# A hybrid decoder layer on one core: another table of turns, and buffers laid out in the order of the record

## The chip, the cores and the metric

The kernel runs on one core of one Trainium2 chip. A core has five engines that run at the same time, each through its own list of instructions strictly from front to back: TensorE (PE in the profile, with its weight loads shown as PEld), VectorE (DVE), ScalarE (ACT), GpSimd (POOL) and SyncE (SP), which here does nothing but issue DMA transfers. An instruction that needs another engine's result, or a buffer that another engine still uses, waits at the head of its list, and everything behind it on that engine waits too.

The metric is device time in microseconds (us) of one execution. A difference of under 0.2% is taken as no change.

## The reference

One layer of a decoder with two groups of heads side by side, 1024 tokens of width 1024, one batch, float32:

```python
h = rms_norm(x, attn_norm_w)
proj = h @ w_in                                  # 1024 x 4496, split into the columns below
(a_q, a_k, a_v, a_z, a_b, a_a, b_q, b_k, b_v, b_z, i_q, i_k, i_w) = split(proj)

# group A: gated DeltaNet, 4 heads of 128
qkv = silu(causal_dwconv([a_q, a_k, a_v]))       # 4 taps
beta, g = sigmoid(a_b), -exp(a_log) * softplus(a_a + dt_bias)
o_a = gated_delta_rule_chunked(l2(a_q), l2(a_k), a_v, g, beta)   # chunks of 64 tokens
o_a = rms_norm(o_a) * silu(a_z)

# group B: sparse attention, 8 heads of 64 over 2 key/value heads
score[t, s] = sum_h i_w[t, h] * relu(i_q[t, h] . i_k[s])         # 8 indexer heads of 128
keep the 256 best causal keys of each token
o_b = softmax(rms(b_q) . rms(b_k) / 8 over the kept keys) @ b_v * silu(b_z)

x = x + [o_a, o_b] @ w_out
gate = sigmoid(rms_norm(x) @ w_gate + b_gate)
x = x + (p @ w_ple) * gate                       # p: 1024 x 256, w_ple: 256 x 1024
```

## The kernel before, in words

**Stages.** The work runs through these stages, which overlap at their borders. In the *head* (about the first 60 us) the input x and a transposed copy of it are loaded in eight blocks of 128 tokens (`xt`, `xc`), each block is normalized, and the product p @ w_ple is formed meanwhile and stored to DRAM in sixteen pieces (`plt` stored to `pled`). Then come the projection columns as a stream of jobs, with the indexer's scores, the search for the 256 best keys and the DeltaNet chunks as chains of work between them. At about 520 us the sparse attention starts, with the rest of the projections and the output projection run between its steps. The last stretch is the second half of the output projection, the gate and the output.

**Products in three passes.** Every large product is made of three matmuls in a rounded format: each operand is split into a high part and a low part, and high x high, low x high and high x low are summed. For a weight piece of 128x512 the raw load is `raww`, the high part `hiw` (cast by ACT, or by DVE for the first piece), the low part `low` (a subtraction on POOL). For p they are `phi` (ACT) and `plo` (DVE, lines 858 to 863), for the normalized x `hThi` and `hTlo`. The product itself is `mm` in PSUM; `ple_out` (lines 878 to 888) copies it to `plt` on ACT and has SP store it.

**Attention.** `kv_load` (lines 1761 to 1767) brings the keys `kst` in eight transfers of 128 tokens each and the values `vst` in one; `load_q` (lines 1777 to 1787) brings the queries of one block of 128 tokens as `Qt`, one transfer, and splits them: ACT writes the two high halves of `qT`, DVE the two low halves. The score product `S` (line 1808) takes `qT` and `kst`, DVE turns it into the masked logits `P` and their minimum `mn`, ACT takes the exponential.

**The end of attention.** The attention's last outputs are transposed and scaled (`ot`), and ACT and POOL split them into `mch` and `mcl` (allocated in `tail_open`, line 1893). These are operands of the output projection's second part, jobs `body` in `out_job` (line 1944), whose result is `g` for the second half of the tokens.

**What sets the order.** None of the calls above reaches an engine at once. `Plan` records each as an `Op` with the earlier ops that it depends on, and each buffer's birth as a mark. `Plan.run` (line 486) then takes the ops in the order that the table `TURNS` gives: 7,561 numbers, packed as text, each the place of the next op among those not yet taken. `Plan.issue` (line 537) issues them in that order, so the table fixes the order of every engine's list, SP's transfers included. Since all recorded work is issued by line 557, the profile shows that line for everything, and one reads it by the names of tiles. The waits between engines come from the dependences and, where a buffer takes memory that another buffer had before, from that reuse.

**Where buffers lie.** A `LatePool` knows all of its buffers when it opens. `lay` sorts them and allocates one after the other; those that hold product operands and fill whole lines of 512 bytes come first, then the rest, and padding keeps the pools' borders on such lines. Which pool's buffer covers which bytes of an earlier pool, and so who waits for whom at reuse, hangs on this order.

Of the kernel before, what the change touches and what calls it, by code (L numbers as in the profile page):

```python
# [79 lines left out]
=7!C{1<aBOxZS|z0!}AzIDp;m1~!`wSY5VEr~H`HSnXCzz6F@gK+5q*mMqC>j+lESNpe{vbDMdoO_EwYlG*IEOLjXjSxnXTI<w6rm0QX!rV_KM&?;F>W|IU=*(OnvU#3Xd  # L80
WHKA&5_}m(lgS92CX>!3&bMH`4Q9Jszd_LJwI+?;Xw+wCXInJ7cwEv&qZ**eH0XjsjY$JCGSmi(pckAb!6pi@+F;U)^H8f@S~;^$2A^e$$KzT)8r4SNuqHE8PzT|FnimA8
!1J8dYUc!tQ4*BAp4TEun+6sHmXGr$o;R>6ol2!vDL9pjb30vDr^4Y-*kPMwu|yQGlqpFeCSYPR5Rqo}T2|}U!Wy-jf*1p%Cyg||Os^mqo?#eP{wX7hpDP%Kq-omnQ<`>5
H0O{w&d70`mZJ?opeTl+Xa!9xm4reL%YO(PMR_TbBw3a<u&ka?DvfGVq0n-2!E#|7I}Zh;n1`fNi3$ayRLWt7QQfOm!Kmf~GUTkZ{DEW$g+fQlr3>V;Wi&x$Q51#AZK5-2
x|^m^it3PK2tp79f*>S<z;OePY2-v0L9j%l97*`(e2eCrh00Xv=^Axr`2NqGuX}rIJ@$+j?7_?+$W+7HZ@>1@*yPv3Z+!o!p`ZOj-`4BR#h>WH?MDg1LlhBtxD!vJm<`Lu
P&6)~Xao(j=sl3A8kK8DS(Qpq@jS0msa#quYv<KgtJ<PAn^{S!udkQ6GbW9Wj+(2hC3b~>*yUm)^XzdJrJX8AjzeWvB@;H4Rb{b+Rc4hGRGIuLpBTJH5U0uEa*0lt#c6d|
?elE2S_j?B@4*^bX$yz7W@|7QwCKWeuuYqjBQ?p$&K4WoS@Y;32D<wDHL++f))VO-F2tDmtc6AQP<anaD?2)(6>a$fO7q;duC5fjOtI-FKjD77Rz`b4Tie9M<m8!&)2BCI
xIjOB5&qjHqf3^YTXOdN#J84=d&VZmn3E^Jdzv}re)0?>zs{V=+$KM$(>D$DldsdXidG-zKK!tc>Fs5D&h^kMR-9h3YSpTvM^_y|mK{F)`pQF(KKkgD70#nakt4KPeO<2O
I7^?qb!*?vORpcnGEmeY<IW?`zxw?1uShRneesPK@0#zvAie&&^yZu9L$~knuSze!^2&h&FTM5}dFMs`?p<>4>#ALEzWEn-cHKS5yz<H$uiSn2-48yv`yXz8_2y0XyZc|=
zkmO?_fy)vq~W4w&S2O`>E5JnpM8b;i2smcDdjvqxPANf`CI3ybJwX?zk%~--h1!mGcVo2UVZgF=JqF_;MXqESFgTy@$Qw2fA@E{uiv?Q_wLP`|K;YJH(y}B%G|tkhrY4q
# [2175 lines left out]
```

## Time and profile before

The median of three runs is 816.04 us (815.69 to 816.8). The profiled execution took 816.13 us; its records span 814.4 us.

| engine | busy us | share of the span |
|---|---|---|
| PE (matmul) | 802.3 | 99% |
| PEld (weight load, beside PE) | 685.0 | 84% |
| DVE | 615.7 | 76% |
| ACT | 572.6 | 70% |
| POOL | 493.2 | 61% |

The DMA engines move 93.14 MB at a mean of 114 GB/s. TensorE's mean granted clock is 0.998 of full speed.

How to read the rows further down: in a timeline each row has its start, its length (both in us), the engine, the line, the operation and `out<-in`; `xN` at the end means N like instructions in one row, and a bracket shows for how long the engine had been idle ahead of it and what ended that. The rows of SP are the issuing of transfers, not their landing. In a table of windows each row has its stretch of time and its length, then the busy time of each engine with its count, TensorE's granted clock, the share of the DMA engines that was busy, and GB/s. Matmuls are pipelined: a 512 wide one is shown with a length of 0.39 us but the next one starts about 0.23 us later, so lost time is read from the starts.

### The profile page before, as it was taken

The numbers are of one execution on the slowest core, as the hardware profiler recorded it, in microseconds if no ns is written. First come the engines' busy times: TensorE is split into PE (matmuls) and PEld (weight loads), VectorE is DVE, ScalarE is ACT, GpSimd is POOL, SyncE is SP. The second block draws the span as 40 slices with busy tenths as digits, with TensorE's granted clock in tenths as the row PEclk, the third lists the DMA queues.
The fourth block names the chain that finished last, engine by engine and source line by source line (L and its number), as shares of the span: only waits on it lengthen the run. The fifth ranks groups of instructions, "written<-read, shape, count | busy, mean of one in ns | idle before, by whom it ended". The sixth has DMA issues, their size and how long they took to land.

```text
span 814.4 us, 14745 instructions
## 1 busy us (share of the span) xinstructions
PE 802.3 (99%) x5111; PEld 685.0 (84%) x5111; DVE 615.7 (76%) x1420; ACT 572.6 (70%) x1317; POOL 493.2 (61%) x670
## 2 busy tenths in 40 slices
PE   8999999999999999999999999999999999999996
PEld 6898889888888888888888888887888888788885
DVE  4654446756778889989999988798868898686577
ACT  6753565555568978988999985498766789886342
POOL 3433514223235765767678775758875478899982
PEclk9999999999999999999999999999999999999999
...
GB/s 289 380 190 105 80 76 53 69 94 65 43 36 38 89 96 55 82 55 103 103 61 48 109 102 104 234 116 234 181 148 137 78 66 52 183 63 79 155 193 130
DMA packets 77866, 93.14 MB, mean 114 GB/s; under 512 B 24000, under 2 KB 40672, under 8 KB 77664
## 3 DMA queue, kind: packets, MB, share of 16 engines
...
## 4 chain that ended last, share of the span: by engine, by line
PE 90%; DMA 3%; ACT 3%; DVE 2%; POOL 1%; issue 1%; SPq 0%; ACTq 0%
PE mm L557 53%; PE g L557 9%; PE s L557 6%; PE lg L557 6%; PE pv L557 4%; PE S L557 4%; PE pt L557 4%; PE rec L557 3%; PE po L557 2%; DMA xt<-in_x_dram 2%; DMA pled<-plt 1%; ACT P L557 1%; DMA Qt<-qd 1%; POOL rs L557 0%; SPq L557 0%
## 5 line engine op out<-in xcount | busy, mean ns | idle before, releaser
L557 POOL TENSOR_TENSOR low<-raww,hiw 128x512 fp32r<-128x512 f32 (+1 forms) x109 | 145.5, 1339 | 130.3 <-ACT hiw L557 124.7
L557 PE MATMUL mm<-hTlo,hiw 128*128 128x512 f32 (+1 forms) x528 | 196.6, 382 | 0.0
L557 PE MATMUL mm<-hThi,hiw 128*128 128x512 f32 (+1 forms) x528 | 195.8, 383 | 0.0
L557 PE MATMUL mm<-hThi,low 128*128 128x512 f32 (+1 forms) x528 | 194.4, 381 | 0.0
L557 PEld LDWEIGHTS mm<-hThi,low 128*128 128x128 f32 x528 | 99.1, 188 | 16.9
L557 PEld LDWEIGHTS mm<-hThi,hiw 128*128 128x128 f32 x528 | 99.1, 188 | 16.1
L557 PEld LDWEIGHTS mm<-hTlo,hiw 128*128 128x128 f32 x528 | 98.9, 188 | 16.2
L557 ACT ACTIVATE junka<-score,nt 128x768 bf16<-128x768 int16 (+5 forms) x96 | 100.0, 1041 | 4.3 <-POOL nt L557 1.5
L557 ACT ACTIVATE hiw<-raww 128x512 fp32r<-128x512 f32 x107 | 66.5, 628 | 25.2 <-PE g L557 8.0
L557 POOL TENSOR_SCALAR P<-P,rsum 128x128 f32<-128x128 f32 (+7 forms) x64 | 50.0, 790 | 37.3 <-DVE rsum L557 36.9
L557 DVE TENSOR_SCALAR_CACHE_REDUCE junk<-score,cand 128x384 bf16<-128x384 f32 (+2 forms) x96 | 71.1, 741 | 1.8
L557 ACT ACTIVATE relu<-lg 128x384 f32<-128x384 f32 (+2 forms) x80 | 40.0, 523 | 44.2 <-PE lg L557 41.6
L557 POOL TENSOR_SCALAR nt<-acca,upa 128x1 f32<-128x1 f32 x96 | 39.7, 416 | 32.0 <-ACT junka L557 28.2
L557 DVE SCALAR_TENSOR_TENSOR score<-relu,sm,score 128x384 f32<-128x384 f32 (+5 forms) x42 | 43.1, 1035 | 16.5 <-ACT relu L557 16.4
L557 ACT ACTIVATE ph<-pt 128x512 fp32r<-128x512 f32 x72 | 41.0, 594 | 18.9 <-PE pt L557 17.4
L557 PE MATMUL S<-kst,qT 128*128 128x384 f32 (+2 forms) x192 | 53.2, 348 | 0.2 <-DVE qT L557 0.2
L557 ACT ACTIVATE P<-P,mn 128x128 f32<-128x128 f32 (+7 forms) x64 | 49.4, 772 | 5.6 <-DVE mn L557 5.0
L557 DVE TENSOR_TENSOR pl<-pt,ph 128x512 fp32r<-128x512 f32 x72 | 47.8, 683 | 6.8 <-ACT ph L557 6.1
L557 ACT ACTIVATE fst<-mm 128x512 f32<-128x512 f32 (+2 forms) x61 | 30.1, 506 | 22.1 <-PE mm L557 18.9
L557 DVE SCALAR_TENSOR_TENSOR acc<-fst,cw,acc 128x512 f32<-128x512 f32 x48 | 37.4, 791 | 10.0 <-ACT fst L557 5.1
L557 PEld LDWEIGHTS S<-kst,qT 128*128 128x128 f32 x192 | 34.6, 188 | 7.0 <-DVE mn L557 0.8
L557 PE MATMUL pt<-ident,P 128*128 128x128 f32 x288 | 40.0, 273 | 0.3 <-DVE pl L557 0.3
...
## 6 DMA issues: line engine op xcount, KB each, us to landing
...
```

The costliest lines, as they stand in the source:

```text
L557: r = getattr(getattr(self.nc, o.eng), fn)(*[real(x) for x in args], **{k: real(v) for k, v in kw.items()})
```

## The change

Two things are changed, and no recorded operation is added, removed or altered.

First, `TURNS` is another table. Second, `lay` sorts a pool's buffers by the place of their birth in the record (`born.i`) and no longer by the turn in which the birth comes up (`turn`). The second moves 153 of 273 buffers to other addresses; names in the rows below that differ only in their number (such as `kst_5459` and `kst_5461`) are the same buffer numbered in the other order.

```diff
 TURNS = r"""
-c-rlG2Xq|AnPzoPGu_iYxu+*5Ou{4#FauzaGeATVBmoc^1i*kyiUbqDAO={>A|;U$DUu>7iXugdNr|FlN?wJP<+LkHw(m~9+ub|w?YldB?bW?o-!*92mTh_Ew{KV8J@b2S
...
+c-rlH2XtK5nclsxmzjBG=1uRtU@#432E7x#vVZ^!dLhvPQmi0AkrYXo6pJj0A}Cf7l*}R)kyN87nbNLgTb8{mTb3OsmScN2@$pG^y*{f=oaBLayt3Aoa}uxZtodQy#lw5^
...
 """
@@
     def lay(self):
-        slots = sorted((s for ring in self.rings.values() for s in ring), key=lambda s: s.turn)
+        slots = sorted((s for ring in self.rings.values() for s in ring), key=lambda s: s.born.i)
         if self.space is not None or self.kw["name"] == "const":
             for s in slots:
                 s.alloc()
```

Engine by engine, the new table leaves the order as it was except in three places: the head (the first 60 us on all engines), the transfers that SP issues just ahead of the attention's first score product, and the stretch from the last blocks of attention to the operand `mch`.

**The head, PE.** The first rows of PE: `xT` are fourteen warming transposes, the `mm` are the products of p and w_ple; `mm_75`, `mm_76` and `mm_77` are the three result buffers, `hiw_106`/`low_107` the first weight piece, `hiw_108`/`low_109` the second, `phi_150`/`plo_151` the split of p. Before:

```order
L557 MATMUL xT_194<-ident_81 128x128 x14
L557 MATMUL mm_75<-phi_150,hiw_106 128x512
L557 MATMUL mm_76<-phi_150,hiw_106 128x512
L557 MATMUL mm_76<-plo_151,hiw_106 128x512
L557 MATMUL mm_76<-phi_150,low_107 128x512
L557 MATMUL mm_76<-phi_150,hiw_106 128x512
L557 MATMUL mm_76<-plo_151,hiw_106 128x512
L557 MATMUL mm_77<-phi_150,hiw_108 128x512
L557 MATMUL mm_76<-phi_150,low_107 128x512
L557 MATMUL mm_75<-plo_151,hiw_106 128x512
```

Now:

```order
L557 MATMUL mm_75<-phi_150,low_107 128x512
L557 MATMUL mm_76<-phi_150,hiw_106 128x512
L557 MATMUL mm_76<-plo_151,hiw_106 128x512
L557 MATMUL mm_76<-phi_150,low_107 128x512
L557 MATMUL mm_76<-phi_150,hiw_106 128x512
L557 MATMUL mm_76<-plo_151,hiw_106 128x512
L557 MATMUL mm_76<-phi_150,low_107 128x512
L557 MATMUL mm_77<-phi_150,hiw_108 128x512
L557 MATMUL mm_77<-plo_151,hiw_108 128x512
```

These nine rows begin with the sixth matmul of `mm_75`: all six of that result now come first, then all six of `mm_76`, and the first that needs the second weight piece (`hiw_108`) stands thirteenth where it stood seventh.

**The head, DVE and SP.** DVE's list now starts with `ident`, and the four small fills that stood ahead of it come later. On SP the stores `pled<-plt` now stand between the loads. Before:

```order
L557 DMA xc_165<-in_xc_dram 128x1024
L557 DMA raww_114<-in_w_ple_dram 128x512
L557 DMA raws_166<-in_w_small_dram 128x1088
L557 DMA pled<-plt_154 128x512
L557 DMA pled<-plt_155 128x512
L557 DMA pled<-plt_156 128x512
L557 DMA raws_167<-in_w_small_dram 128x1088
```

Now:

```order
L557 DMA xc_164<-in_xc_dram 128x1024
L557 DMA pled<-plt_154 128x512
L557 DMA raww_114<-in_w_ple_dram 128x512
L557 DMA pled<-plt_155 128x512
L557 DMA raws_165<-in_w_small_dram 128x1088
L557 DMA pled<-plt_156 128x512
L557 DMA pled<-plt_154 128x512
L557 DMA raws_166<-in_w_small_dram 128x1088
```

The load of the third weight piece (`raww_114`) and those of the small projections' weights (`raws`) are now queued behind stores that wait for ACT's `plt`.

**The attention's start, SP.** The transfers ahead of the first score product; `mixd<-z` are stores of group A's output, `raww` weight pieces, `zd<-fst` a store of a projection. Before:

```order
L557 DMA mixd<-z_2456 128x512
L557 DMA kst_5459<-kd 128x4x128
L557 DMA raww_114<-in_w_ct_dram 128x512
L557 DMA Qt_5470<-qd 128x4x128
L557 DMA kst_5459<-kd 128x4x128 x2
L557 DMA Qt_5471<-qd 128x4x128
L557 DMA kst_5459<-kd 128x4x128
L557 DMA raww_115<-in_w_ct_dram 128x512
L557 DMA zd<-fst_129 128x512
```

Now:

```order
L557 DMA mixd<-z_2457 128x512
L557 DMA raww_114<-in_w_ct_dram 128x512
L557 DMA kst_5461<-kd 128x4x128 x4
L557 DMA Qt_5474<-qd 128x4x128
L557 DMA Qt_5477<-qd 128x4x128
L557 DMA raww_115<-in_w_ct_dram 128x512
L557 DMA zd<-fst_128 128x512
```

The first `Qt` stood behind one `kst` and one `raww`; it now stands behind that `raww` and four `kst`, so three transfers of keys have gone in front of it. On PE nothing moved here: the first `S` follows the same matmul as before.

**Near mch, PE.** The last matmuls of one output projection job (`mm`, with operand `m0B`) and the first `g` that reads `mch`. Before:

```order
L557 MATMUL mm_76<-m0Bh_5846,hiw_108 128x512
L557 MATMUL mm_76<-m0Bl_5847,hiw_108 128x512
L557 MATMUL mm_76<-m0Bh_5846,low_109 128x512
L557 MATMUL g_7362<-mch_5848,hiw_110 128x512
L557 MATMUL g_7363<-mch_5848,hiw_108 128x512
```

Now:

```order
L557 MATMUL mm_75<-m0Bh_5846,hiw_108 128x512
L557 MATMUL mm_75<-m0Bl_5847,hiw_108 128x512
L557 MATMUL g_7363<-mch_5848,hiw_112 128x512
L557 MATMUL mm_75<-m0Bh_5846,low_109 128x512
L557 MATMUL g_7362<-mch_5848,hiw_110 128x512
L557 MATMUL g_7365<-mch_5848,hiw_108 128x512
```

One `g` has moved ahead of the job's last matmul.

More of the change, by code (lines that the diff above doesn't have):

```diff
@@ L82 @@
[L82 to L89, printed above, removed]
@@ new lines @@
+13&Qje8B4k9uIK4fy?UxPA70W{0@iL;c>YgE{D_Yl#6Vq!vXAZr(M3$X^+~0&E|KsJ8X8h-EMO=*_=*wox|z^Rkmus&9}r?Zt<2_Jw;YfWHGyQ&1SPB<#3qonHICd9I;!>
+)~FR&{C2y^=C|2Qp8L()7aNzGcQ^|5mi&B+K6erNoE$Sq>TE!()0<)jBcju5b&^)H>2w~Q*_q*Vp46G5I-SvA{v{-nNuNyWv!$%8EFF@Op-ChXh$d#xsnc~Dv&M@WMYUek
+iAK?k2u71yt5s{ATCF5WS@L0$B)ufpFNCGEKqwRl3IVm?^C4at0^;Vayd7w)CXG?UaXJo$B*}LFLzy&6wN<B9uP~`KYJ*y@)~SFbiGo^bj3_ymUjH$tbLez(zs)-CC!F5G
+aVD)=Qmb`3rB;+Ag<36$GQ6VbQz`{cL#vhYp9-T*5VXP_K_ke}>jj-gtJO%NMo_CoQ7H&AD-;69^Lkz(cZid_C2$<4=0vec6jg$X-_5J!3zUji_V;s2J*ChB7Gq=pnx<nk
@@ new lines @@
+?T`_2{1O$k-6PKgnd`(H4#I9H?n8GVOb{53V}V7;)Ju<KWOQ_n-Tl&6-+S-d-~Z7+0*IjYaC%AW(8PwhD|i0s=StoliB_%bJ)Mo!VsQ+^BJzPzG+l`0kYo~DtPRib%h&W6
+rp2(J2J>S+5yJ$G=Xnw1IG(!?!Kqe>HqmMoE#l(r*4Nj|<(PSNbktH+Wmc^V4!Yf{sA~~L`7U0jD(~QvnRedBTdfh^!kg20Q;-iB(~OI7nVfF7(X~i7mrJIb)iLNBu=UH3
+`YaYpx-}fOrKP1=wUNl0h}0%!XE&Rhnwqk*j18WQMXc>3*Y@-zG_fwcGukm&sOZQ0`uYls?qkV)tX#5cRji^dPsA93dwA{IlxnqN`%iz${ryH6?FDUZ6BCn@=O)gcoqp~)
+=GlwLk6TAuTNhf-Uzqr-)^YFH<QRME)VI#EXFR9RvGT8T=hDwUeC`~5`>g&RbDCjzMm^7c_+dBO)x~x$bTaGKon1FHH1xz1Lyx1YAA9VL^+%5#J9c%Q>xn1O#~HQy1-XrR
+)dlAE?MH82e&camHo9KM-6yZVcK!OR=2x!0^yW+VEcaeCzww6ot+y;k@7xt$Gr#ictA`K2{QB$E-Is)W_o#z!@O$5S>l=6X-aEp+`s$mn-uv>GKltF@zrXdxTeno-I`rD1
@@ new lines @@
+Lx=wQ5G@^~^cOXAdi^$9`xbrY{Hyf0g%4>Jtz5(hckbM|aQgzi@WNgCYlLv_-FII(_wrr*wb$Nd?|l3*apN*`?b_=X?_GTUCqKFK!rgoK?%lfegIjOidXfDid+YLD=H`YE
+n7iM&h2FVy^ZE;}XP>37Ub+0@h1-|DeC@*38yBxXf9?6J3fg|z&WbE6oK>7TbK~tZfBBbRIP=_dSFT)n^Ude(T{iy3vuDnqIrE0`^qFT*y?TMZw6JjU41eMD*;A)(<m=B|
+J@fnv^QG6X&(9yfas2xHwOhAty*+>P=JDh8PaQx0)KlMo>Z6Y?UHOlfjvv2y;<@jBm-*<UW5*X37LIivJ9qBbv(GXYo>*Yce-)wr3-#oa`X`P)eq#RIxpPO4QaXX==N$)l
+mJ=vOX*@D#Jai>#ytH@LIJ<xLz^>2D%+1}oGdDN$^8OQ9v!_m-+PmY-40Y<?Q75-wJA2lvIz78}=IN(ZC$>y~X?n}s$G-gK)2H7#_Ab47W@d(2*reGmZDf7Eug?{Jf7188
@@ new lines @@
+eFqOdF|oxrH-6-r?<#d;<0GS2@ef9>?0RS5osqYD-hQv^z4zW52@lU)9v*pkc<0Uw!wVzB!=uA;adz|YrcEPH51$yne_?)Pa(F_<=RZF&H8pW~<k<Mg!Qsb89~-_ta&7o3
+ap=jRt7Aupjt&hyOc0c62NhOOA*$=?O>AeNW5<&not;~+cgST&$I*@>M;@P=>X_{58Q;)Dt)<5I(R=C3XX!I@bQ?jPZ~f}v%7KA_+18oIcJ*T`W}OFTcH_&Ib<RG5%LBx}
+y&PZmO?+w7ww75LO*1olS2Qi(Eu(4IUKyr|#zs@a+=hmknT9PxyLRo}{z$`~^K)}^OVe5g8k!p#8Yg$x@2Wp_ss(SZYpQFktHU3!#UIljZMck2RXzG#Rc%#O^?~Y%xw)$S
+4J}n8RXgh%cUBcu;YTVDA3j{Q9ot%oZQE3_rAwnRIyD-^rYp$LFDxv~N0;R<%|pjg)95HVf+p+G>}>gyg=SWv8A}os6%|r>0?mwNpwW0#9W5*<h~%Sr$=qBjo|R6<GGgIy
@@ L148 @@
+fq$s3|7lhK$8fJ-lX?`VC~EPadmiA=EW$ld_6PWb2pRl+)C52C3jCc9!vBNLz|ZUi{Ovd4znZE;@cXVB{_9LO{H@yZna26V#KBKl82%~`hQDC~;QxLC{_eSipQ!7TjDVk&
+w|tr~5Po845dJRi!B6xQ{#N?_;tqtrnS1{-kNW4X!`~|Dzuq4FOqco1*WjnhPgM4)!TfrI@Yk#g!LQjF{`1MdoX1bm2L5h82EW~^@YAcPPw)$V#!Q0;G4a7}%m442IVg%@
+1VQ{M*dG3oCmTK>^aDJQ&j<K7Ch_nA*&g5lJ`?{7P$I>B
 """
```

112 lines of the change are left out of this document (50 added, 62 removed).

## The prediction

> **What bounds the kernel now.** I read the page first, then the chain, then PE's stretches.
>
> ```profile
> span 814.4 us, 14745 instructions
> PE 802.3 (99%) x5111; PEld 685.0 (84%) x5111; DVE 615.7 (76%) x1420; ACT 572.6 (70%) x1317; POOL 493.2 (61%) x670
> PE 90%; DMA 3%; ACT 3%; DVE 2%; POOL 1%; issue 1%; SPq 0%; ACTq 0%
> ```
>
> PE is busy for 99% of the span and makes up 90% of the chain that ended last. No instruction is added or removed, so PE's own work cannot change; only the time in which PE waits can. Where that is, a table of windows tells:
>
> ```profile
> 0.00:36.00 36.00, 31.88 (x157) 25.64 (x158) 17.75 (x36) 23.61 (x43) 13.13 (x24) 1.00 0.94 325
> 60.00:500.00 440.00, 439.93 (x3230) 379.84 (x3228) 337.82 (x801) 322.24 (x807) 237.67 (x422) 1.00 0.25 74
> 500.00:530.00 30.00, 29.84 (x160) 25.20 (x159) 22.78 (x51) 15.53 (x45) 20.12 (x21) 1.00 0.64 209
> 700.00:720.00 20.00, 18.72 (x85) 14.68 (x85) 11.20 (x17) 15.44 (x28) 18.02 (x15) 1.00 0.53 184
> 720.00:814.40 94.40, 88.25 (x408) 73.28 (x406) 67.62 (x108) 45.06 (x80) 76.30 (x61) 0.98 0.38 126
> ```
>
> In the first 36 us PE is idle for 4.12 us (36.00 less 31.88), some of it before its first instruction, and there the DMA engines are 0.94 busy. From 60 to 500 us it is idle for 0.07 us, where the order is unchanged. Around 522 us it loses 0.16 us and around 705 us 1.28 us. After 720 us its busy time is short by 6.15 us, which is the store of the last results after PE's last matmul and moves with it. So the change can act in three places, the three where the order moves: it can take something off the head's 4 us or add to it, and it can open a hole around 520 us or close the one at 705 us. Since PE never catches up, each microsecond of hole is a microsecond of the end.
>
> **The head.** PE's rows, then those of DVE, ACT and SP that release them:
>
> ```profile
> 4.96 0.90 PE L557 MATMUL mm<-phi,hiw 128*128 128x512 f32 x2
> ...
> 7.18 0.49 PE L557 MATMUL mm<-plo,hiw 128*128 128x512 f32 x1
> 8.43 0.50 PE L557 MATMUL mm<-phi,hiw 128*128 128x512 f32 x1 [0.76 <-ACT hiw L557]
> ```
>
> ```profile
> 1.79 0.21 DVE L557 TENSOR_SCALAR ident<-jp 128x128 f32<-128x128 f32 x1
> 4.29 0.49 DVE L557 CAST hiw<-raww 128x256 fp32r<-128x256 f32 x2 [2.29 <-DMA raww<-in_w_ple_dram]
> 4.70 1.24 DVE L557 TENSOR_TENSOR plo<-xt,phi 128x512 fp32r<-128x512 f32 x1
> 6.43 0.69 DVE L557 TENSOR_TENSOR plo<-xt,phi 128x512 fp32r<-128x512 f32 x1 [0.49 <-ACT phi L557]
> ```
>
> ```profile
> 7.75 0.63 ACT L557 ACTIVATE hiw<-raww 128x512 fp32r<-128x512 f32 x1 [1.35 <-DMA raww<-in_w_ple_dram]
> ```
>
> ```profile
> 9.62 0.58 ACT L557 ACTIVATE plt<-mm 128x512 f32<-128x512 f32 x1
> ```
>
> ```profile
> 6.56 0.33 SPq L557 DMA_DIRECT2D raww<-in_w_ple_dram  x1
> ```
>
> DVE reaches `ident`, for which the fourteen transposes wait, at 1.79, behind four fills. With `ident` in front the transposes end sooner, but the first `mm` also needs `hiw`, half of the cast that starts at 4.29 (two in 0.49 us, so done at about 4.54). The first `mm` then comes at about 4.65 where it came at 4.96: 0.3 us gained.
>
> Next, before, six matmuls start up to 7.18 and the seventh waits for ACT's `hiw` (7.75 plus 0.63 is 8.38) until 8.43. That start is 1.02 us after the normal 0.23 us step. The new list has twelve matmuls that do not need this `hiw`. They wait for `plo` instead: the first `plo` takes 1.24 us and can start at 4.54, so the second matmul waits until about 5.85, some 1.0 us after its turn; the second `plo` ends at 7.12 as before and costs another 0.4 us. Twelve steps of 0.23 us (2.8) from 4.65 plus 1.4 us of waits end at about 8.8 us, where the list before has done eight. By then PE is four to five matmuls ahead, 1.0 us.
>
> What becomes of this lead is less clear. The third `raww` was issued at 6.56 and now stands behind a store that waits for `plt`, the copy on ACT which ended at 10.20 (9.62 plus 0.58); with the lead that is about 9.2, so the load is some 2.6 us later. And the later waits are set by the loads of x:
>
> ```profile
> 31.68 1.06 ACT L557 ACTIVATE sq<-xt 128x1024 bf16<-128x1024 f32 x1 [1.23 <-DMA xt<-in_x_dram]
> ```
>
> ```profile
> 33.37 0.50 PE L557 MATMUL mm<-phi,hiw 128*128 128x512 f32 x1 [0.95 <-ACT plt L557]
> ```
>
> The largest one, at 33.37, where PE stood 1.11 us, ends with ACT's `plt`, and ACT had reached that copy late because the operation ahead of it, `sq`, had waited for a load of x. With the DMA engines 0.94 busy in this stretch, x cannot land much earlier for being asked for earlier. So part of the lead is given back as longer waits for x. I take a gain of 0.7 us for the head. The bounds: a gain of 2.1 us (the lead of 1.0 stays, and the 1.11 us at 33.37 goes as well) and a loss of 0.6 us (the lead is given back and the late third weight piece costs one more wait as long as the 0.6 us step of an ACT copy).
>
> **The attention's start.** SP's rows before, and the chain from the first `Qt` to the first `S`:
>
> ```profile
> 514.04 0.57 SPq L557 DMA_DIRECT2D kst<-kd  x1
> 514.71 0.56 SPq L557 DMA_DIRECT2D raww<-in_w_ct_dram  x1
> 515.33 0.42 SPq L557 DMA_DIRECT2D Qt<-qd  x1
> 515.80 1.23 SPq L557 DMA_DIRECT2D kst<-kd  x2
> 517.08 0.62 SPq L557 DMA_DIRECT2D Qt<-qd  x1
> 517.74 1.61 SPq L557 DMA_DIRECT2D kst<-kd  x1
> ```
>
> ```profile
> 515.33 4.77 DMA Qt<-qd
> 520.12 0.64 ACT qT L557
> 520.78 0.69 DVE qT L557
> 521.50 0.70 DVE qT L557
> 522.25 0.50 PE S L557 x2
> ```
>
> ```profile
> 521.70 0.39 PE L557 MATMUL mm<-hThi,low 128*128 128x512 f32 x1
> ```
>
> ```profile
> 522.69 0.63 ACT L557 ACTIVATE qT<-Qt 64x512 fp32r<-64x512 f32 x1 [0.76 <-DMA Qt<-qd]
> ```
>
> ```profile
> 514.00:524.10 10.10, 9.94 (x47) 8.05 (x46) 4.90 (x10) 4.05 (x10) 7.31 (x7) 1.00 0.90 279
> ```
>
> `Qt` was the third of these transfers. It landed at 520.10, and ACT, DVE and PE followed without a pause, 2.15 us in all, to the first `S` at 522.25. PE's matmul ahead of it started at 521.70, so PE stood 0.32 us beyond its step: the first `S` was already set by `Qt`, and there is no cover left. Behind that `S` on PE's list stand all further matmuls, which therefore wait as well.
>
> Now `Qt` is the sixth of these transfers, all of 256 KB, with three `kst` put in front. Three ways to price that. The sixth one of before was the second `Qt`, for which ACT waited until 522.69, so the sixth landed at about 522.66 (ACT starts 0.02 to 0.03 us after a landing, as at 520.12), 2.56 us after the third. By bandwidth: at the 279 GB/s of this stretch 256 KB take 0.94 us, three 2.8 us. From below: `Qt` is issued in the place where the second `Qt` was, at 517.08, 1.75 us later, and if its 4.77 us to landing did not grow it would land 1.75 us later. I take 2.5, nearest to the landing of the sixth, which has the same make-up of transfers ahead of it, with bounds of 1.75 and 2.8. The hole then is 2.5 us wider. The four `kst` land earlier than they did, which helps nobody: the first `S` needs one of them and waited for `qT`. What is late next, DVE's `mn` and ACT's exponentials, moves along with the `S` that feed them.
>
> **Near mch.**
>
> ```profile
> 704.87 0.39 PE L557 MATMUL mm<-m0Bh,low 128*128 128x512 f32 x1
> 706.50 1.47 PE L557 MATMUL g<-mch,hiw 128*128 128x512 f32 x4 [1.25 <-ACT mch L557]
> ```
>
> PE stood 1.41 us beyond its step until ACT's `mch` came. With one `g` ahead of the last `mm`, the wait starts 0.23 us sooner and ends at the same event, and the matmul that went behind is done after it: nothing in sum. What it covers is a second wait just behind: the row at 706.50 holds four matmuls in 1.47 us, where three steps of 0.23 and a last one of 0.39 make 1.08, so some 0.3 us more were waited among them. I take a gain of 0.1 us, with bounds of 0.3 either way.
>
> **Addresses.** 153 buffers have moved, which adds and removes waits for reuse: the load of `vst` now waits for PE also. SP issues it at the end of this same stretch, after the second group of `Qt`, and PE reads it only in the blocks after that. I take nothing for it, since the rows that would pay, SP's gaps, lie beside PE's stream; the widest gap there is the 1.61 us of SP on a `kst`, and if `vst` held SP that long its bytes would still be on time.
>
> **The sum.** 816.13 us of the profiled execution, less 0.7, plus 2.5, less 0.1: 817.8, a change of +1.7. The median of the runs lies 0.09 us under the profiled execution, so **817.7 us**.
>
> **A rule on the clock.** The hole grows from about half a microsecond to about 3 us from start to start, which makes 2.66 us in which PE has nothing in it (521.70 and 0.39 end at 522.09; 522.25 and 2.5 are 524.75). What does TensorE's clock do then? The end of the program shows it:
>
> ```profile
> 808.00:809.00 1.00, 0.25 (x3) 0.04 (x1) 1.00 (x3) 0.62 (x2) 0.02 (x1) 1.00 0.55 211
> 810.00:811.00 1.00, 0.00 (x0) 0.00 (x0) 0.79 (x3) 0.45 (x1) 0.24 (x1) 0.95 0.00 0
> 811.00:812.00 1.00, 0.00 (x0) 0.00 (x0) 0.42 (x1) 0.00 (x0) 0.00 (x0) 0.50 0.88 327
> ```
>
> PE's last matmul ends in the first of these windows, after 0.25 us, at 808.25. The granted clock is 1.00 until somewhere in the second: 0.95 is nine tenths of a microsecond at full clock and one tenth at half. So it fell to 0.50 at about 810.9, 2.65 us after the last matmul. The hole that I forecast is as long. The Trainium skill, in "TensorE: Matmul & The Clock Gate", section "Part 1: The HAM clock gate", says that a free-running window of about 3.4 us without enough work halves the clock, and that a busy window of the same length brings it back. By that rule a hole of 2.66 us alone is shorter than a window and the clock would mostly hold; the row says that a window with some work at its start can fall too. No hole of before is long enough to decide it.
>
> **The rivals.**
>
> *The head pays for it (816.2).* The head gains its upper bound, 2.1 us, `Qt` costs its lower one, 1.75, mch 0.1: -0.4 us; with values halfway to these from mine (1.4 and 2.1) +0.6. Their middle is +0.1. For it: the head's 4.12 us of idle time are more than the hole costs. Against it: 0.94 of DMA in that stretch. Between 815.6 and 816.7.
>
> *Not slower, since the keys do not delay Qt (815.2).* The mechanism: the sixteen DMA engines take transfers side by side, so that a `Qt` queued behind four `kst` lands when its own bytes are through, no later than before. Its place is the first `qT` on ACT; it decides if `Qt` lands before 520.8 or so. Then only the head and mch remain, -0.8 us. For it: transfers overlap, since the first `Qt` takes 4.77 us and SP issues one every 0.6 us. Against it: the time to landing grows with the place in the queue, 4.77 us for the third, 5.6 for the sixth, as in a queue that is served in turn.
>
> *The clock falls in the hole (819.0).* If the granted clock goes to 0.50 around 524 us for a stretch as long as the 2.65 us that it took to fall, half of that stretch, 1.3 us, is lost on top of the forecast. For it: the row above. Against it: the hole must reach its full forecast length at a moment that suits. By the rule of "TensorE: Matmul & The Clock Gate" in the Trainium skill the slow stretch would be one window of 3.4 us, an estimate of 1.7 us lost and 819.4 us.
>
> *The change does not do what it says*, in that the new addresses give new waits that reorder nothing but slow everything. Against it: the order of each engine, read from the two programs, differs only in three places. Times from 816.5 to 820; I give it 4 in 100.
>
> **How the numbers follow.** The forecast has 0.48, the head that pays 0.18, the keys that do not delay 0.13, the clock 0.17, addresses 0.04. The forecast's own range is 816.4 to 818.9: the bounds of its terms (-2.1 to +0.6, +1.75 to +2.8, -0.3 to +0.3) do not fall to one side together. The range for 8 in 10 reaches to the other cases on both sides: 815.4 to 819.6. A difference of 0.2%, 1.6 us, is about what a measurement of this kernel can tell from no change, so slower begins at 817.7 and faster lies below 814.4. The forecast lies on that border and gives 0.25 to slower and 0.23 to within; the clock and the addresses are slower (0.21); the head that pays is within (0.16), but for 0.02 in which the head gains more than its bound and the whole is faster; of the keys that do not delay, whose 815.2 lies 0.8 us from the other border, 0.07 is within and 0.06 faster. That makes faster 0.08, same 0.46, slower 0.46.
>
> **What would show it.** In the changed kernel's timeline the first `mm` of the head should start near 4.65 and PE should show no wait for the second `hiw`, but two for `plo` before 7.3 us; the first 36 us should have about 32.5 us of PE busy time or the same x loads should end the waits. `Qt` should land sixth and 2.5 us later against PE's stream, with PE's row for the first `S` showing 2.5 to 3 us of idle time released by DVE's `qT`. At mch PE should stand about 1.6 us. The granted clock between 522 and 530 us settles the third rival. The forecast is wrong if the first `S` follows its matmul within a microsecond, or if PE's idle time in the first 60 us has grown.

## The result and the profile after

The changed kernel takes **823.11 us** (median of 4 runs, 821.29 to 825.15); the kernel before, run beside it, 816.10 us (4 runs, 815.69 to 816.8). The ratio is 1.0086, with a 95% interval of 1.0059 to 1.0112: 7.0 us slower. The forecast was 817.7 us with a range up to 819.6. The profiled execution of the changed kernel took 823.94 us and its records span 822.2 us, 7.8 us more than before.

The table of windows of the changed kernel (stretch and length, busy time of PE, PEld, DVE, ACT and POOL with counts, TensorE's granted clock, DMA share, GB/s):

```profile
0.00:36.00 36.00, 33.63 (x169) 26.89 (x170) 18.69 (x36) 24.64 (x44) 14.41 (x25) 1.00 0.91 329
500.00:535.00 35.00, 31.72 (x159) 26.86 (x158) 23.14 (x58) 16.38 (x44) 20.41 (x24) 0.95 0.53 177
535.00:700.00 165.00, 164.73 (x886) 139.62 (x885) 138.30 (x364) 133.34 (x280) 113.87 (x110) 1.00 0.38 124
700.00:730.00 30.00, 25.59 (x119) 19.98 (x118) 20.82 (x26) 20.64 (x38) 25.81 (x21) 0.98 0.48 158
```

Two of these stretches of the kernel before, which were not shown yet:

```profile
500.00:535.00 35.00, 34.84 (x189) 29.55 (x188) 27.31 (x69) 19.24 (x57) 23.36 (x28) 1.00 0.66 211
700.00:730.00 30.00, 28.72 (x132) 22.95 (x132) 21.06 (x32) 23.79 (x43) 28.02 (x23) 1.00 0.41 141
```

PE is busy for 1.75 us more in the first 36 us, for 3.12 us less around the attention's start and for 3.13 us less around 715 us. In both of the last two the granted clock is also below 1.00, so the matmuls that were done there took longer as well. From 535 to 700 us PE is busy for 164.73 us, before for 164.72. So there is one hole where the forecast put it, and a second one that it did not have.

**The first hole**, in PE's timeline:

```profile
520.19 0.39 PE L557 MATMUL mm<-hThi,low 128*128 128x512 f32 x1
523.85 0.78 PE L557 MATMUL S<-kst,qT 128*128 128x256 f32 x2 [3.28 <-DVE qT L557]
525.28 0.63 PE L557 MATMUL mm<-hThi,low 128*128 128x512 f32 x1
...
527.38 0.40 PE L557 MATMUL mm<-hThi,hiw 128*128 128x512 f32 x1
```

The first `S` follows its matmul after 3.66 us, 3.11 us more than the 0.55 us of before. Behind it the 512 wide matmuls are shown with 0.63 us and start 0.43 us apart; before the hole it was 0.39 and 0.23, and the granted clock is 0.50 from 523.91 to 527.32 us. At 527.38 the normal step is back. SP's rows, and a piece of the chain that ended last, show what came late:

```profile
512.99 2.60 SPq L557 DMA_DIRECT2D kst<-kd  x4
515.62 1.30 SPq L557 DMA_DIRECT2D Qt<-qd  x2
```

```profile
515.62 6.09 DMA Qt<-qd
```

`Qt` is issued 4.57 us ahead of the last matmul (520.19 less 515.62), where before it was 6.37 (521.70 less 515.33): 1.80 us later. And it takes 6.09 us to land where it took 4.77: 1.32 us more. That makes 3.12 us.

**The stretch near mch** starts as before. PE waits for `mch` for 1.63 us beyond its step (before 1.40), but with one matmul of 0.23 us still to do behind the wait that it had done ahead of it before, so nothing is lost here:

```profile
707.77 0.39 PE L557 MATMUL mm<-m0Bl,hiw 128*128 128x512 f32 x1
709.63 0.50 PE L557 MATMUL g<-mch,hiw 128*128 128x512 f32 x1 [1.47 <-ACT mch L557]
```

**The second hole** comes 15 us later:

```profile
724.73 0.39 PE L557 MATMUL mm<-mch,sl 128*128 128x512 f32 x1
728.06 0.50 PE L557 MATMUL g<-mch,hiw 128*128 128x512 f32 x1 [2.93 <-DVE t1l L557]
729.40 0.63 PE L557 MATMUL g<-mcl,hiw 128*128 128x512 f32 x1
...
732.96 0.62 PE L557 MATMUL g<-mch,hiw 128*128 128x512 f32 x2
```

PE stands 3.10 us beyond its step until DVE's `t1l`, and from 728.71 to 732.12 us the granted clock is 0.50 again, with a step of 0.43 us. DVE's rows ahead of it, and POOL's in the same time:

```profile
720.15 0.75 DVE L557 SCALAR_TENSOR_TENSOR h1Al<-g,g,h1Ah 128x512 fp32r<-128x512 f32 x1 [0.16 <-ACT h1Ah L557]
720.82 4.50 DVE L557 SCALAR_TENSOR_TENSOR m0Bl<-x,g,m0Bh 128x512 fp32r<-128x512 f32 x1
...
727.32 0.68 DVE L557 TENSOR_TENSOR t1l<-g,t1h 128x512 fp32r<-128x512 f32 x1
```

```profile
720.93 1.32 POOL L557 TENSOR_TENSOR low<-raww,hiw 128x512 fp32r<-128x512 f32 x1
722.19 1.32 POOL L557 TENSOR_TENSOR mixl<-v,mixl 128x512 f32<-128x512 f32 x1
723.44 1.33 POOL L557 TENSOR_TENSOR sl<-mixl,sh 128x512 fp32r<-128x512 f32 x1
726.13 1.03 POOL L557 TENSOR_TENSOR r<-r,mhalf 128x4 f32<-128x4 f32 x1 [1.36 <-DVE r L557]
```

`m0Bl` is the low part of an operand of the output projection, one DVE operation on 128x512 numbers with two tensors in SBUF, `x` and `m0Bh`. It is shown with 4.50 us. During all of it POOL runs `low`, `mixl` and `sl`, one directly after the other (1.26 us from start to start), and `m0Bl` ends 0.55 us after the last of them (723.44 and 1.33 are 724.77; 720.82 and 4.50 are 725.32). Behind `m0Bl` on DVE stand four operations and then `t1l`, for which PE waits. How unusual the 4.50 us are, the groups of DVE operations by their tile say (count, then min/median/max in ns), of the kernel before:

```profile
L557 DVE SCALAR_TENSOR_TENSOR m0Bl<-x,g,m0Bh x4: 737/1126/1368, 705.0 to 722.5; 128x512 fp32r<-128x512 f32 x4
```

and of the changed one, with another frequent DVE operation of this size below it:

```profile
L557 DVE SCALAR_TENSOR_TENSOR m0Bl<-x,g,m0Bh x4: 742/1574/4498, 708.1 to 728.6; 128x512 fp32r<-128x512 f32 x4
L557 DVE TENSOR_TENSOR pl<-pt,ph x72: 669/684/694, 532.7 to 704.6; 128x512 fp32r<-128x512 f32 x72
```

`pl<-pt,ph` reads one tensor from PSUM and one from SBUF; in 72 times, most of them beside POOL, it never takes more than 694 ns.

In sum, for the two profiled executions: head -1.5 (the matmul ahead of the first `S` starts at 520.19, before at 521.70), first hole +3.1, half clock behind it +1.55, mch 0, second hole +3.1, half clock behind it +1.6: +7.85 us, of 7.8 measured. The 1.55 us is worked out below; the 1.6 us is the time from 728.63 to 732.50, 3.87 us for ten matmuls that take 2.3 at 0.23 us each.

### The profile page after: what moved, and what is told of

It reads as the page before. It is cut to its first block, busy times and chain, and to the rows that moved or that the text cites. A ratio compares the mean times of both kernels' runs of the same rounds, so it can differ in the third digit from the quotient of the medians.

```text
span 822.2 us, 14743 instructions
## 1 busy us (share of the span) xinstructions
PE 805.8 (98%) x5111; PEld 687.0 (84%) x5111; DVE 620.3 (75%) x1420; ACT 573.1 (70%) x1317; POOL 494.9 (60%) x670
## 4 chain that ended last, share of the span: by engine, by line
PE 92%; DVE 3%; ACT 3%; DMA 1%; issue 1%; SPq 0%; POOL 0%; DVEq 0%
PE mm L557 55%; PE g L557 9%; PE s L557 6%; PE lg L557 6%; PE pv L557 4%; PE S L557 4%; PE pt L557 4%; PE rec L557 3%; PE po L557 2%; DMA Qt<-qd 1%; ACT P L557 1%; DVE g L557 0%; DMA xt<-in_pT_dram 0%; SPq L557 0%; DVE qT L557 0%
```

## Experiments

All are the kernel before or the changed kernel with the table, the sorting or a line altered. Ratios are to the kernel before on the same chip, with a 95% interval. In the diffs of order, rows are one engine's list, without the buffers' numbers.

### Addresses and order apart

`addr_only` has the new sorting (`born.i`) with the old table, `order_only` the new table with the old sorting (`turn`).

> The old table with buffers laid out in the order of the record. Theory (order): 816.1 us within 0.5, PE's rows as before. Rival (addresses): 2 to 5 us slower, with at least one hole of PE that the kernel before does not have.

> The new table with buffers still laid out by turn. Theory (order): the whole loss comes from the order, so it is as slow as the changed kernel, 821 to 825 us, with the first S some 3.3 us late and matmuls at half clock behind it, and with a second hole near 725 us behind one DVE instruction of 4.5 us. Rival (addresses): the long DVE instruction comes from where its buffers lie now; then it takes 0.75 to 1.4 us here, the second hole is gone and the time is 818 to 819 us.

Measured: `addr_only` 815.99 us, ratio 1.0003 (0.9993 to 1.0012); `order_only` 824.88 us, 1.0118 (1.0097 to 1.0138). The addresses cost nothing that can be measured; the order costs all. The profile of `order_only` has both holes, and `m0Bl` with 4.46 us in it.

### The three places one by one

`att_only` is the kernel before with nothing new but SP's transfers at the attention's start:

```diff
 DMA mixd<-z 128x512
-DMA kst<-kd 128x4x128
 DMA raww<-in_w_ct_dram 128x512
+DMA kst<-kd 128x4x128 x4
 DMA Qt<-qd 128x4x128
-DMA kst<-kd 128x4x128 x2
 DMA Qt<-qd 128x4x128
-DMA kst<-kd 128x4x128
 DMA raww<-in_w_ct_dram 128x512
```

> The old table but for SP's seven transfers at the attention's start, which are in the new order. Theory (hole and clock): the first S comes 2.6 to 3.1 us later than before and the clock falls to 0.50 behind it, which costs 1.2 to 1.5 us more: 820.0 to 820.7 us. Rival (hole alone): the matmuls behind the hole run at full speed, 818.7 to 819.2 us. Rival (the forecast's size): 818.5 us.

Measured: 819.74 us, ratio 1.0051 (1.0036 to 1.0066), which is +4.2 us. PE's timeline:

```profile
521.02 0.39 PE L555 MATMUL mm<-hThi,low 128*128 128x512 f32 x1
524.02 0.50 PE L555 MATMUL S<-kst,qT 128*128 128x256 f32 x2 [2.61 <-DVE qT L555]
524.87 0.63 PE L555 MATMUL mm<-hThi,low 128*128 128x512 f32 x1
...
528.24 0.40 PE L555 MATMUL mm<-hTlo,hiw 128*128 128x512 f32 x1
```

The hole is 2.45 us wider than before (3.00 from start to start, before 0.55). The clock is still full for the first matmuls and falls at about 524.8, after 2.61 us with nothing in PE (521.41 to 524.02) and 0.75 us of work. It comes back at 528.2.

`head_only` and `head_exact` have the new lists in the head alone, the same on every engine, but merged among the engines in two ways (the first after the old table's order of the engines, the second after the new one's). The first rows of DVE stand for them:

```diff
 UNCONDITIONAL_BRANCH
-MEMSET fst 128x512
-MEMSET sel 64x1
-MEMSET ones 128x128
-TENSOR_SCALAR tri<-jp 128x128
 TENSOR_SCALAR ident<-jp 128x128
```

> The old table but for the head, which is in the new order on all engines. Theory: 1.5 us faster than before, 814.6 us, since PE reaches the matmul ahead of the first S 1.5 us sooner in the changed kernel. Rival (given back later): the chain that loads Qt does not move with PE, the first S stays where it was, and the gain is 0.3 us or less: 815.8 us.

> The old table with the new table's own rows for the head, in their own interleaving. Theory: 0.6 to 1.5 us faster than before, 814.5 to 815.4 us. Rival: no gain, 816.0 us.

Measured: `head_only` 815.45 us, 0.9994 (0.9985 to 1.0003); `head_exact` 816.44 us, 1.0002 (0.9992 to 1.0011). Both theories had the head faster by more (814.6, and 814.5 to 815.4 us). Eleven runs of `head_exact` lie between 814.2 and 817.2, 29 runs of the kernel before beside it between 814.4 and 817.8. So the head has no gain that these runs can tell from nothing; by the intervals it lies between a gain of 1.2 and a loss of 0.9 us.

`tail_only` and `tail_exact` have the new lists near mch alone, merged in the same two ways. DVE's list, in part:

```diff
 SCALAR_TENSOR_TENSOR m0Bl<-x,g,m0Bh 128x512
 TENSOR_TENSOR mm<-x,mm 128x512
-SCALAR_TENSOR_TENSOR m0Bl<-x,g,m0Bh 128x512
 SCALAR_TENSOR_TENSOR mixl<-mm,g,b 128x512
...
 SCALAR_TENSOR_TENSOR h1Al<-g,g,h1Ah 128x512
+SCALAR_TENSOR_TENSOR m0Bl<-x,g,m0Bh 128x512
+SCALAR_TENSOR_TENSOR g<-g,g,b 128x512
+TENSOR_SCALAR r<-mm 128x4
```

> The old table but for the stretch from the last attention blocks to mch, which is in the new order on all engines. Theory: the second hole comes from this stretch alone, since DVE's m0Bl now stands where POOL has three instructions in a row ready: 819 to 821 us, with a hole of about 3 us and half clock behind it. Rival (shift): the hole needs the delay from the attention's start, and this kernel is within 0.5 us of 816.1.

> The old table with the new table's own rows for the stretch from the last attention blocks to mch, in place and in their own interleaving of the engines (the earlier kernel for this stretch was interleaved anew, which gave ACT a wait for DVE that neither table has). Theory: the loss of this stretch is the DVE instruction m0Bl that waits beside POOL, so PE has no hole before 707 us, one of about 3 us (with half clock behind it) some 17 us after the mch wait when m0Bl is held up, and one under 0.6 us when it is not: 820 to 821 us, or 816.3 us. Rival (the stretch is slow for another reason): the holes near 695 and 699 us of the earlier kernel stay.

Measured: `tail_only` 820.74 us, 1.006 (1.0045 to 1.0075). That is the theory's 819 to 821 us, but by luck, and it says nothing on the change: by the way in which the lists were merged, ACT waits for DVE's `mixl` at 693.38 for 2.21 us, a wait that neither kernel has, and `m0Bl` is at most 1.36 us long. `tail_exact`, without it: 816.45 us, 1.0007 (0.9998 to 1.0016), eleven runs of 815.5 to 817.8. In its profile `m0Bl`, at the very place in DVE's list that it has in the changed kernel, takes 1.26 us:

```profile
717.49 1.26 DVE L555 SCALAR_TENSOR_TENSOR m0Bl<-x,g,m0Bh 128x512 fp32r<-128x512 f32 x1
```

```profile
716.90 1.30 POOL L555 TENSOR_TENSOR sl<-mixl,sh 128x512 fp32r<-128x512 f32 x1
718.16 1.75 POOL L555 TENSOR_TENSOR low<-raww,hiw 128x512 fp32r<-128x512 f32 x1
```

Here `m0Bl` came in at the first change of POOL's operations, and it was POOL's next one that took longer, 1.75 us in place of 1.30. So the place in the list is not enough for the 4.5 us.

By the ratios the three are +0.2, +4.2 and +0.6 us (`head_exact`, `att_only`, `tail_exact`): +5.0 of 7.0. The 2.0 us between are no more than the intervals of these ratios allow; what the traces show beyond the three parts is the long `m0Bl`, which `tail_exact` does not have.

### How long a hole halves the clock

`att_1kst` and `att_2kst` are `att_only` in smaller steps: one `kst`, and two, moved ahead of the first `Qt`.

```diff
 DMA raww<-in_w_ct_dram 128x512
+DMA kst<-kd 128x4x128
 DMA Qt<-qd 128x4x128
-DMA kst<-kd 128x4x128 x2
+DMA kst<-kd 128x4x128
 DMA Qt<-qd 128x4x128
```

> The kernel before with the first Qt behind one more kst (two kst and the raww ahead of it). Theory (each kst is worth its landing, and the clock falls only behind a long hole): the first S comes 0.9 us later, no half clock: 816.8 us. Rival (the clock falls behind any hole over a microsecond): 818 us.

> The kernel before with the first Qt behind two more kst. Theory (landing): the first S comes 1.8 us later, and PE has nothing in it for some 2.0 us; if the clock holds, 817.7 us; if the gate already falls at 2.0 us, 819.0 us.

Measured: `att_1kst` 817.09 us, 1.0015 (1.0006 to 1.0024); `att_2kst` 817.87 us, 1.0029 (1.0019 to 1.0038). PE of the first and of the second:

```profile
521.49 0.39 PE L555 MATMUL mm<-hThi,low 128*128 128x512 f32 x1
522.66 0.50 PE L555 MATMUL S<-kst,qT 128*128 128x256 f32 x2 [0.79 <-DVE qT L555]
524.64 0.39 PE L555 MATMUL mm<-hThi,hiw 128*128 128x512 f32 x1
```

```profile
521.81 0.39 PE L555 MATMUL mm<-hThi,low 128*128 128x512 f32 x1
524.55 0.50 PE L555 MATMUL S<-kst,qT 128*128 128x256 f32 x2 [2.36 <-DVE qT L555]
524.90 0.58 PE L555 MATMUL mm<-hTlo,hiw 128*128 128x512 f32 x1
...
528.55 0.39 PE L555 MATMUL mm<-hThi,hiw 128*128 128x512 f32 x1
```

The hole grows to 1.17 and to 2.74 us from start to start, by 0.62 and 2.19 us (expected 0.9 and 1.8). With one `kst` the clock stays. With two it fell in the profiled execution, which took 820.08 us, after 2.36 us with nothing in PE. Of the eleven runs three (819.52, 820.08, 821.2) have a mean granted clock of 0.996, the other eight (817.26 to 818.33) 0.998 to 0.999. So with a hole of this size it depends on the execution; on what, is worked out further down.

These traces also price the half clock. In `att_1kst`, the twelve matmuls from the first `S` up to the one at 524.64 take 1.98 us. The same ones take 3.53 in the changed kernel (523.85 to 527.38): 1.55 us lost. In `att_only` and `att_2kst` the same comparison, over the matmuls up to the end of the slow stretch, gives 1.54 and 1.56.

`after_fill` takes the suspected cause away: the changed kernel, with twelve transposes of the identity put on PE ahead of the first `S`. They write to the PSUM buffer of that `S` before its product does.

```diff
+            if o.eng == "tensor" and o.parts[0][1][0].t.tag == "S" and not count.get("warm"):
+                count["warm"] = 1
...
+                for _ in range(WARM_S):
+                    r = self.nc.tensor.transpose(o.parts[0][1][0].t.get()[:, :128], ident, ident)
```

> The changed kernel with twelve transposes of ident (2.7 us of PE) put ahead of the first S, into the PSUM buffer that this S overwrites; they run while PE would wait. Theory (clock gate): PE is not idle there, the clock stays at 1.00 behind the first S, and the time is 1.2 to 1.5 us less than the changed kernel's 823.1: 821.7 us. Rival (the slow matmuls have another cause, such as kst or qT being read while transfers land): they stay at 0.43 us from start to start, and the time is 823.1 us.

Measured: 821.83 us, 1.008 (1.0049 to 1.0111), in two groups of three: 818.61 to 819.83, with a mean clock of 0.998 to 0.999, and 823.82 to 827.41, with 0.992 to 0.996. That the median is the theory's 821.7 is luck: it lies between the groups, where no run is. The profiled execution is one of the first group (819.83). Its PE and its window:

```profile
522.28 1.47 PE L556 MATMUL S<-ident 128*128 128x128 f32 x12
525.30 0.50 PE L564 MATMUL S<-kst,qT 128*128 128x256 f32 x2 [1.55 <-DVE qT L564]
525.64 0.40 PE L564 MATMUL mm<-hTlo,hiw 128*128 128x512 f32 x1
```

```profile
500.00:535.00 35.00, 33.45 (x183) 28.49 (x182) 24.94 (x60) 17.67 (x51) 21.93 (x25) 1.00 0.57 187
```

The transposes keep PE busy for 1.47 us, not for 2.7, and leave 1.55 us empty. `Qt` still comes late, and the first `S` starts 3.26 us after the last matmul of the projections, but the clock is 1.00 and the steps behind are normal. So it is the empty time, not the late operand, that halves the clock. What lowered the clock in the upper group, for which there is no profile, is open.

### The operation on DVE

`after_m0bl` is the changed kernel with `m0Bl` moved behind `t1l` on DVE, and nothing else:

```diff
 SCALAR_TENSOR_TENSOR h1Al<-g,g,h1Ah 128x512
-SCALAR_TENSOR_TENSOR m0Bl<-x,g,m0Bh 128x512
 SCALAR_TENSOR_TENSOR g<-g,g,b 128x512
...
 TENSOR_TENSOR t1l<-g,t1h 128x512
-SCALAR_TENSOR_TENSOR m0Bl<-x,g,m0Bh 128x512 x2
+SCALAR_TENSOR_TENSOR m0Bl<-x,g,m0Bh 128x512 x3
```

> The changed kernel with one DVE instruction, the m0Bl that took 4.5 us, moved five places down DVE's list, behind t1l. Theory (POOL holds a port that this instruction needs): g, r, gth and t1l ahead of it, which read PSUM, run at once, the hole near 725 us shrinks from 3.1 to under 0.5 us and the clock does not fall there: 818.0 to 819.0 us. Rival (DVE is late for another reason): the hole stays, 822 to 824 us.

Measured: 821.34 us, 1.0062 (1.005 to 1.0074), five runs of 820.09 to 822.23. The second hole is gone, as the theory said: the longest wait of PE from 722 to 740 us is one of 0.26 us. The time is not: it lies 2.3 us above the theory's 819.0. Its range is about the changed kernel's median less the 4.7 us of the second hole and its half clock; but `att_only`, which has no second hole, had measured 819.74, and short waits between 731 and 740 us, behind the moved operation, cost some 1.3 us here. The hole before the first `S` and its half clock remain (window 500 to 535 us: 32.45 us busy, clock 0.95).

`after_again` is the changed kernel once more, to see how often `m0Bl` is held up.

> The changed kernel once more, unaltered. Theory (m0Bl is held up in some executions and not in others): times in two groups, 819 to 820 and 822.5 to 825 us, and if the profiled execution falls in the lower group its m0Bl takes under 2 us and the hole near 725 us is under 0.6 us. Rival (m0Bl is always held up): one group, and a profile with m0Bl at about 4.5 us at every time.

Measured: 822.40 us, 1.0076 (1.006 to 1.0093), in two groups: 820.08, 820.21 and 821.36, and 823.44 to 824.15. The profiled execution is of the second group (823.44), and `m0Bl` takes 4.45 us in it:

```profile
720.34 4.45 DVE L557 SCALAR_TENSOR_TENSOR m0Bl<-x,g,m0Bh 128x512 fp32r<-128x512 f32 x1
```

The lower group lies where `after_m0bl` lies. Of the five profiles of kernels that have the new order in this stretch with the rest of the table, three show about 4.5 us (changed kernel, `after_again`, `order_only`) and two 1.9 us: `after_fill`, and the next one. In all five `m0Bl` starts 0.08 to 0.11 us ahead of POOL's `low`, so a shift between the two engines does not tell the cases apart.

`after_qt_back` is the changed kernel with the old transfers at the attention's start, the reverse of the diff of `att_only`.

> The changed kernel with the seven transfers at the attention's start in the old order again. Theory (m0Bl is held up only where the earlier hole has shifted POOL against DVE): m0Bl takes under 2 us, no hole over 0.6 us near 725 us, and the time is 816.4 us. Rival (the stretch near mch brings the hold-up by itself once the new addresses or the new head are there): two groups of times, 816.4 and 820 to 821 us.

Measured: 817.7 us, 1.0027 (1.0009 to 1.0046), and eleven runs spread from 814.59 to 823.29, which is neither the theory's 816.4 nor the rival's two groups. Taking the first hole away alone brings the ratio from 1.0086 to 1.0027, 4.8 us of 7.0. In the profiled execution, 817.23 us, there is no hole at 522 us, and `m0Bl` takes 1.92 us. It took no more with the first hole in `after_fill` (1.95 us), so the late `Qt` does not bring the hold-up by itself. The runs up to 823.29 us are not explained by any profile: that they are executions with `m0Bl` held up is likely from the size, but it was not seen.

### Two attempts at something faster

`head_qt_first` is the kernel before with the new head and with `Qt` as the first of the transfers; `best2` adds to it that the last product of `ot` goes to DVE, since PE waits for its result `mch`.

```diff
+DMA Qt<-qd 128x4x128
 DMA kst<-kd 128x4x128
 DMA raww<-in_w_ct_dram 128x512
-DMA Qt<-qd 128x4x128
```

```diff
-                nc.gpsimd.tensor_tensor(ot, ot, zt, op=OP.mult)
+                (nc.vector if i == 7 else nc.gpsimd).tensor_tensor(ot, ot, zt, op=OP.mult)
```

> The kernel before with the new order of the head alone, and with the first Qt put ahead of all kst and raww on SP. Theory: the head's gain of 1.5 us and the 0.3 us that PE stood ahead of the first S: 814.3 us. Rival: the first S waits for raww or kst instead of Qt, or a weight piece is late, and it is 814.6 us or more.

> The kernel before with the new table's rows for the head, the first Qt ahead of kst and raww on SP, and the last block's product of ot and zt on DVE (0.7 us) instead of POOL (1.29 us), which is in the chain to mch. Theory: 1.0 us from the head, 0.3 from the first S, 0.6 at mch: 814.2 us. Rival (mch is bound elsewhere): 814.8 us or more.

Measured: `head_qt_first` 815.46 us, 0.9991 (0.9983 to 1.0000); `best2` 816.0 us, 0.9999 (0.9991 to 1.0008). In `best2` PE's wait for `mch` fell from 1.40 us to 0.74 (`mm` at 704.76, `g` at 705.73), and still nothing came of it: its runs lie between 814.33 and 817.48. Both times lie in their rivals' ranges; in the profile of `best2` the head has gained nothing (521.89 for the matmul ahead of the first `S`, before 521.70). No version was found that beats the kernel before by more than can be measured.

## Why the prediction was wrong

**Where time can be lost** was right: PE's record lost time in the head, at the attention's start and in the last stretch, and nowhere else.

**The head**, forecast -0.7 us, is near 0 (`head_exact` +0.2, with -0.7 to +0.9; `head_only` -0.5), which does not refute the term. The rows of PE in the changed kernel:

```profile
4.69 0.65 PE L557 MATMUL mm<-phi,hiw 128*128 128x512 f32 x1
6.49 0.49 PE L557 MATMUL mm<-phi,hiw 128*128 128x512 f32 x1 [0.19 <-ACT phi L557]
7.21 0.50 PE L557 MATMUL mm<-plo,hiw 128*128 128x512 f32 x1 [0.23 <-DVE plo L557]
```

The first `mm` starts at 4.69 (forecast 4.65) and there is no wait for `hiw`. The waits for `plo` were smaller than forecast: the second matmul starts at 5.20 (forecast 5.85), and the one wait for `plo` shown is 0.23 us. The twelfth starts at 9.04, before at 9.70: a lead of 0.66 us where 1.0 was forecast. The wait at 33.37 us is gone as well, and the profiled execution gained 1.5 us. What the forecast lacked is that this is not so in each execution. In the profiles of `order_only` and `after_qt_back` the matmuls run at the half clock up to about 10.2 us (shown with 0.74 to 0.80 us at first, then a step of 0.43), where those of the changed kernel are shown with 0.50 or less from 5.20 on; their twelfth matmul starts 1.7 and 1.5 us later than the changed kernel's. And in `after_fill`, `head_exact`, `best2` and `head_qt_first` PE waits for ACT's `sm` between 27 and 29 us, for 1.16, 0.87, 0.76 and 0.34 us, a wait that the profiles of the changed kernel and of before do not have.

**`Qt` behind three `kst`**, forecast +2.5 with bounds of 1.75 and 2.8: the wider hole measured 2.34 us in `order_only`, 2.45 in `att_only`, 2.53 in `after_again` and 3.11 in the profile of the changed kernel, the only one beyond the bound. The term was right. It is made of the two things that the forecast used as alternatives: the issue is 1.8 us later, and the time to landing grows too, by 0.55 us (`order_only`, 5.32) to 1.32 (the changed kernel, 6.09). So the rival in which keys do not delay `Qt` falls, and so does the rival in which the head pays.

**The clock** is the first step that failed. The forecast took its hole of 2.66 us without a matmul to leave the clock alone and gave the other case 0.17. The half clock came in each of the five profiles with `Qt` behind all `kst` and nothing put into the hole, after 2.51 us (`order_only`), 2.55, 2.61, 2.69 and 3.28 of empty PE. By the mean clock it did not come in each run: 823.71 us of `order_only`, 820.21 of `after_again` and 821.58 of `after_m0bl` have 0.998 to 1.000, the other runs of these kernels 0.993 to 0.997. Its price was 1.55 us, between the rival's two prices of 1.3 and 1.7. The rival's terms for `Qt` and the clock, 2.5 and 1.3, make 3.8 us, and `att_only`, where nothing else was changed, lost 4.2. Had this been the likeliest case, the forecast would still have been too low.

What the row at the end of the program showed (clock down 2.65 us after the last matmul) was one sample of a varying time. The clock fell 2.3 us after the last matmul's end in `after_m0bl`, 2.7 in `att_2kst`, 3.4 in `att_only` and 3.7 in `order_only`, in the last three with matmuls running again. The traces show why it varies. In each of them the clock changes only on a grid of 3.41 us: in the changed kernel it falls at 523.91 and at 728.71 us, 204.80 us apart, which is 60 times 3.413, and each half-clock stretch is one step of that grid. What decides is how much of one such stretch PE is empty, not how long the hole is. Two holes of one length tell it, that of `order_only` from 726.07 to 728.96 (2.89 us) and that of `after_again` which ends at 727.52 (2.88 us). Windows cut along the grid, of `order_only`:

```profile
723.81:727.22 3.41, 2.26 (x10) 1.52 (x9) 3.41 (x4) 0.29 (x1) 2.05 (x3) 1.00 0.85 227
727.22:730.63 3.41, 1.67 (x7) 1.41 (x8) 3.41 (x5) 2.89 (x6) 2.26 (x2) 1.00 0.66 234
```

and of `after_again`:

```profile
725.63:729.04 3.41, 1.52 (x7) 1.26 (x8) 3.41 (x5) 3.05 (x6) 2.26 (x2) 1.00 0.60 218
729.04:732.45 3.41, 3.41 (x10) 2.64 (x9) 3.40 (x6) 2.45 (x5) 2.35 (x3) 0.50 0.00 0
```

In `order_only` the hole lies across two stretches, empty for 1.15 and 1.74 us (3.41 less PE's busy time), and the clock stays at 1.00. In `after_again` one stretch is empty for 1.89 us, and the next runs at 0.50. Ahead of the eight falls between 520 and 730 us in the profiles, in `att_2kst` and in the five profiles with the late `Qt`, the stretch was empty for 1.89 to 3.28 us; behind the first 12 us no profile has a fall after a stretch that was empty for 1.74 us or less. So a hole such as the forecast's, 2.66 us, may pass or not by where it meets the grid.

This fits the rule of the Trainium skill, "TensorE: Matmul & The Clock Gate", section "Part 1: The HAM clock gate", of a free-running window of about 3.4 us, better than the forecast's reading of it. The page's table lets the clock fall after an idle window; here a window in which PE was busy for 1.52 us was enough, and the measurement decides.

**Near mch** is the second step that failed, and the larger error. The forecast said that one `g` had moved ahead of a job's last `mm`, "nothing in sum", and took -0.1 us with bounds of 0.3 either way. At that place this held: PE stood 1.63 us there where 1.6 were forecast. But the step looked at one engine at one spot. The third place in which the order differs does not end with `mch`, as the text ahead of the prediction has it: the lists of PE, DVE, ACT and SP differ up to about 730 us. There one DVE `m0Bl` had moved from behind `mm<-x,mm` to a place behind `h1Al` and ahead of `t1l`, the operation that the matmuls need next; and POOL works there without a gap from 709.7 to 724.8 us. At the new place it cost up to 3.1 us of hole and 1.6 us of half clock in the executions in which POOL kept its turn, and some 0.7 us in the others (`after_fill`, `after_qt_back`). No case of the forecast held this, so the range did not either.

The profile of before had a trace of it. DVE's rows around `m0Bl`, and POOL's of the same moment:

```profile
708.36 1.25 DVE L557 SCALAR_TENSOR_TENSOR m0Bl<-x,g,m0Bh 128x512 fp32r<-128x512 f32 x1 [1.42 <-ACT m0Bh L557]
709.53 0.74 DVE L557 SCALAR_TENSOR_TENSOR mixl<-mm,g,b 128x512 f32<-128x512 f32 x1
712.96 0.70 DVE L557 TENSOR_TENSOR g<-x,g 128x512 f32<-128x512 f32 x1 [2.69 <-PE g L557]
```

```profile
709.02 1.75 POOL L557 TENSOR_TENSOR ssum<-ssum,mixl 128x512 f32<-128x512 f32 x1
```

Of these, `m0Bl` and POOL's `ssum` are each 0.45 to 0.5 us longer than their kind is alone (0.74 and 1.29 us). Behind `m0Bl` stood one operation, and then DVE was idle for 2.69 us: had it been held up here, most of that would have been covered. The move took this cover away. The Trainium skill, "SBUF — State Buffer", section "SBUF: two separate sides", says that a DVE operation with two inputs in SBUF and a GpSimd operation that reads SBUF exclude each other, and whoever starts first keeps the port for its whole instruction. The rows agree with it, and `pl`, which has only one input in SBUF, is never prolonged. They show one thing more: a DVE operation that waits does not get its turn at the next change of POOL's operations for certain. In the changed kernel `m0Bl` missed the changes at 720.93, 722.19 and 723.44 and came in only when POOL had no next operation ready; in `after_fill` and `after_qt_back` it came in at the second change, and in `tail_exact`, where it starts 0.67 us ahead of the change and not 0.1, at the first. What decides this is open. That it is this port was not tried by itself, for example by feeding `m0Bl` from PSUM; shown are the overlap in time, the hole that goes when `m0Bl` stands elsewhere, and the two groups of times.

**Addresses**, forecast 0: right, by `addr_only`.

The sum by what was measured: head 0, `Qt` +2.5, half clock +1.55, near mch +0.7 where `m0Bl` comes in early and up to 4.8 in the executions in which it is held up. That is 820.8 us for the ones and about 825 for the others, and the runs of the changed kernel lie between 820.1 and 825.2.
